# A differential-attention block: subtracting the two softmax maps in one step, and normalising the output per query in its own partition

## The chip, the cores and the metric

The kernel runs on one NeuronCore of a Trainium2 chip. The metric is the device time of one execution in microseconds (us). The engines named below are PE (TensorE: matmuls and transposes), DVE (VectorE), ACT (ScalarE), POOL (GpSimd) and SP (SyncE, which only issues DMAs here). Each engine takes its own list of instructions strictly in order.

## The reference

The program is one transformer block over 1024 tokens of width 1024: three attention branches (A: differential attention, B: dilated windows, C: attention to a memory), gates, an output projection and a feed-forward part. The change is in branch A, which has 4 heads; each head has two softmax maps over all 1024 keys, and values of width 128:

```
s = jnp.einsum('bqhcd,bkhcd->bhcqk', qb, k).astype(jnp.float32) * scale
s = s - slopes[None, :, None, None, None] * dist[None, None, None]
p = jax.nn.softmax(s, axis=-1)
p_diff = p[:, :, 0] - lam * p[:, :, 1]
return jnp.einsum('bhqk,bkhe->bqhe', p_diff.astype(v.dtype), v)
...
out_a = diff_attention(aq, ak, av, slopes_a, lam)
out_a = (rms_norm(out_a, a_subln[l]) * (1.0 - lambda_init)).reshape(b, t, BRANCH_WIDTH)
```

`rms_norm` divides each query's 128 outputs by the root of their mean square plus 1e-6, so a factor that is common to all outputs of a query only matters beside that 1e-6.

## The kernel before

The program runs in stages: the projections (to about 604 us of the profile), branch C (to about 685 us), branch A (about 685 to 1006 us), branch B (to about 1270 us), then mixing, output projection and feed-forward.

Branch A works on **steps**: one head and one block of 128 queries, 32 steps in all. Two steps (the index `e`) make a **pair** of 256 queries, 16 pairs in all. One step does this:

- For each of the two maps `m`: PE makes scores `sp` in two halves of 512 keys (L740, L741); three PSUM banks hold them. DVE adds the distance and takes the running minimum (L742), writing the row tile `s` (128 queries x 1024 keys). ACT takes the exponential in place and sums the row into `alc` (L746).
- DVE forms the reciprocals `arl` of both sums (L750) and multiplies the second by minus lambda, `nlam` (L751). POOL scales the second map by it (L752). DVE scales the first map and adds the second (L753).
- PE transposes the difference in 8 blocks into `tp` (L759); ACT, POOL and DVE split the transposed map into a high and a low part `pt` (L762, L765, L766, L768).

After both steps of a pair, PE multiplies with the values: 24 matmuls into the PSUM tile `op` (L773 to L775), with the 128 value columns in the partitions and the 256 queries along the row. The norm then needs a sum over partitions, per query. ACT copies `op` to `au` and squares it to `asq` (L778, L779). PE multiplies a matrix of ones with `asq`, so that each query's sum of squares stands in all 128 partitions (L781). The helper `rsqrt` takes its inverse root on tiles of 128x256: logarithm and exponential on ACT (L91, L92), one Newton step on DVE (L93 to L95). DVE multiplies `au` by it (L783), and a DMA stores `au` to DRAM (L784). `opp`, the pool that holds `op` and the sums of squares, has a single PSUM bank.

Between all this a filler runs: the gate projections, in units of 12 matmuls (tile `mm`, L191 to L193, called gate matmuls below), whose weights are loaded by SP, prepared by ACT and POOL (L210, L211), and whose results DVE takes out of PSUM (L542 to L574). The call `some_gates` releases one unit per step in branch A; a later stage takes what is left. A scheduler sets the final order of every engine's list when the program is built, and it may move instructions between neighbouring steps and stages; the lists are fixed after that.

At the start of branch B, SP loads three bias tables (L794) and then projected rows `nat` (L287), which PE transposes first (L293, 16 in a row). These loads stand behind the last store of `au` in SP's list.

Of the kernel before, what the change touches and what calls it, by code (L numbers as in the profile page):

```python
# [10 lines left out]
F32 = mybir.dt.float32  # L11
# [3 lines left out]
AF = mybir.ActivationFunctionType  # L15
ALU = mybir.AluOpType
# [4 lines left out]
P = 128  # L21
D = 1024
T = 1024
# [6 lines left out]
EPS = 1e-6  # L30
# [47 lines left out]
def hybrid_block_kernel(ctx: ExitStack, tc: tile.TileContext, xT, memT, w_ab, w_cq, w_kv,  # L78
                        w_gate, w_br, w_out, w_fg, w_fu, w_fd, pk_d, strip_d, bias0_d, bias1_d, bias2_d, out):
    nc = tc.nc  # L80
# [7 lines left out]
    def rsqrt(tp, val, n, shape, names, bufs=None):  # L88

        z, t = (tp.tile(shape, F32, name=m, bufs=bufs) for m in names)  # L90
        nc.scalar.activation(t, val, AF.Ln, bias=cst[:, {64: 0, 128: 1, D: 3}[n]:][:, :1])  # L91
        nc.scalar.activation(z, t, AF.Exp, bias=cst[:, 2:3], scale=-0.5)  # L92
        nc.vector.tensor_mul(t, z, z)  # L93
        nc.vector.scalar_tensor_tensor(out=t, in0=val, scalar=n * EPS, in1=t, op0=ALU.add, op1=ALU.mult)
        nc.vector.scalar_tensor_tensor(out=z, in0=t, scalar=1.5, in1=z, op0=ALU.subtract, op1=ALU.mult, reverse0=True)  # L95
        return z
# [7 lines left out]
    const = pool("const")  # L104
    ident = const.tile([P, P], F32, name="ident")
    make_identity(nc, ident)
    pk = const.tile([P, PK_COLS], F32, name="pk")
    nc.sync.dma_start(out=pk, in_=pk_d)
    cst = const.tile([P, 4], F32, name="cst")
    for i, v in enumerate((64 * EPS, 128 * EPS, -0.5 * math.log(2.0), D * EPS)):  # L110
        nc.vector.memset(cst[:, i:i + 1], v)
    ones = const.tile([P, P], F32, name="ones")
    nc.vector.memset(ones, 1.0)
# [4 lines left out]
    gk = const.tile([P, 8], F32, name="gk")  # L118
    for i, (a, b, dh) in enumerate(((PK_AQ, PK_AK, 64), (PK_BQ, PK_BK, 128), (PK_CQ, PK_CK, 128))):
        nc.vector.scalar_tensor_tensor(out=gk[:, i:i + 1], in0=pk[:, a:a + 1], scalar=-2.0 * float(dh) ** 0.5,  # L120
                                       in1=pk[:, b:b + 1], op0=ALU.mult, op1=ALU.mult)
# [9 lines left out]
    nlam = lams[:, 3:4]  # L131
# [38 lines left out]
    opp = pool("opp", 1, PSUM, att)  # L170
    small = pool("small", 3, stack=att)

    def ps_tile(pl, name):
        return pl.tile([P, 512], F32, name=name)
# [143 lines left out]
    with ExitStack() as pst:  # L318
# [61 lines left out]
        sq = sqs[0]  # L380
# [280 lines left out]
    with ExitStack() as st:  # L661
# [58 lines left out]
        for h in range(AH):  # L720
            QS, KA, KB = qk
            vH, vL = values(h)
            for pair in range(4):
                if h < AH - 1:
                    if pair == 0:
                        ahead = queries_keys(h + 1)
                    for _ in range(A_AHEAD[pair]):
                        qk = next(ahead)
                pts = [[ap.tile([P, 4, 256], F32R, name="pt", bufs=4) for _ in "HL"] for _ in range(2)]
                for e in range(2):  # L730
                    n = 2 * pair + e
                    off = (11 - (8 * (n % 2) + n // 2)) * 64
                    pr, lc = [], small.tile([P, 2], F32, name="alc")
                    for m in range(2):
                        tt = ap.tile([P, T], F32, name="s4", bufs=4)
                        nm = small.tile([P, 2], F32, name="anm")
                        for ch in range(2):
# [8 lines left out]
                        nc.scalar.activation(tt, tt, AF.Exp, bias=nm[:, 1:2], scale=-1.0, accum_out=lc[:, m:m + 1])  # L746
                        pr.append(tt)
                    some_gates(A_FIRST + (8 * h + 2 * pair + e + 1) * A_STEP, last, A_LAG)
                    rl = small.tile([P, 2], F32, name="arl")
                    nc.vector.reciprocal(rl, lc)  # L750
                    nc.vector.tensor_mul(rl[:, 1:2], rl[:, 1:2], nlam)  # L751
                    nc.gpsimd.tensor_mul(pr[1], pr[1], rl[:, 1:2].broadcast_to([P, T]))  # L752
                    nc.vector.scalar_tensor_tensor(out=pr[0], in0=pr[0], scalar=rl[:, 0:1], in1=pr[1],  # L753
                                                   op0=ALU.mult, op1=ALU.add)
                    for hf in range(2):
                        tp = ps_tile(tpp, "tp")
                        for k in range(4):
# [19 lines left out]
                sq = ap.tile([P, 256], F32, name="asq")  # L777
                nc.scalar.copy(u_, op)  # L778
                nc.scalar.activation(sq, op, AF.Square)  # L779
                ms_ = ps_tile(opp, "op")[:, :256]  # L780
                nc.tensor.matmul(ms_, lhsT=ones, rhs=sq, start=True, stop=True)  # L781
                y = rsqrt(ap, ms_, P, [P, 256], ("subz", "asq"))
                nc.vector.scalar_tensor_tensor(out=u_, in0=u_, scalar=gk[:, 3:4], in1=y, op0=ALU.mult, op1=ALU.mult)  # L783
                nc.sync.dma_start(out=spill[0][:, h, pair * 256:(pair + 1) * 256], in_=u_)  # L784


# [604 lines left out]
```

## Time and profile before

| | |
|---|---|
| median of 3 runs | 2114.03 us (2113.95 to 2117.42) |
| the profiled execution | 2113.94 us, its span 2112.2 us |
| busy share of the span | PE 94%, weight loads 81%, DVE 65%, POOL 53%, ACT 43% |
| PE idle over the span | 2112.2 - 1991.7 = 120.5 us |

Each engine's busy time is the union of its instructions' spans, so 100% would be an engine that never waits. Matmuls are pipelined: a 512-column matmul is shown as about 0.39 us long, while the next one starts 0.23 us after it. Shares over the whole span average over stages with different limits; branch A is about 15% of the span and is read by itself below. Times in the rows are counted from the span's start.

### The profile page before, as it was taken

To read this page: it belongs to the slowest core of one execution; us is meant where nothing else is said; L and a number is where in the kernel's file an instruction comes from. 1 tells how busy PE (TensorE), PEld (TensorE's weight loads), DVE (VectorE), ACT (ScalarE), POOL (GpSimd) and SP (SyncE) were. 2 spreads that over 40 slices of the span, in tenths; PEclk is the share of its full clock that TensorE was granted. 3 is DMA by queue.
4 is the path that set the end of the run, shared out by engine and by line. 5 is a ranking of instruction groups with operands and counts; after the bars stand their busy time and mean duration, and the time that the engine had idled before them with its cause. 6 is when DMAs were issued, how large, how long until landed. Compare 5 with 4: busy or idle time off the path is not lost. (4 is left out here: it accounts for less than half of the span.)

```text
span 2112.2 us, 31356 instructions
## 1 busy us (share of the span) xinstructions
PE 1991.7 (94%) x11384; PEld 1719.1 (81%) x11384; DVE 1367.5 (65%) x2144; ACT 917.2 (43%) x1839; POOL 1129.0 (53%) x770
## 2 busy tenths in 40 slices
PE   6799999999999889899989997999999999999999
PEld 5799999999977667678767785777788888888887
DVE  8975533566575799996354436733977667579961
ACT  4444322344444566664544555522523332344441
POOL 5686644666643576665355324810166454545754
PEclk9899999999999999999999998999999999999999
DMA  6263343323143333244856437632344323255442
GB/s 227 77 221 108 105 149 107 102 92 127 71 165 130 128 108 93 92 170 148 284 194 218 165 112 289 209 125 80 129 142 157 102 90 125 95 166 223 148 147 70
DMA packets 134730, 300.37 MB, mean 142 GB/s; under 512 B 19120, under 2 KB 43184, under 8 KB 134064
## 3 DMA queue, kind: packets, MB, share of 16 engines
q1 hardware_dynamic: 134576, 298.37, 41.9%
q8 instruction: 90, 1.47, 0.3%
q14 instruction: 64, 0.52, 0.1%
HBM read 204.58 MB, written 89.54 MB: 139 GB/s over the span
## 5 line engine op out<-in xcount | busy, mean ns | idle before, releaser
L211 POOL TENSOR_TENSOR wl<-raw,wh 128x512 fp32r<-128x512 f32 x204 | 282.2, 1396 | 190.8 <-ACT wh L210 167.2
L191 PE MATMUL pb<-t,wh 128*128 128x512 f32 x795 | 309.3, 391 | 15.6 <-DVE t L1100 14.5
L192 PE MATMUL pb<-t,wh 128*128 128x512 f32 x795 | 310.7, 391 | 1.9 <-DVE t L260 1.9
L193 PE MATMUL pb<-t,wl 128*128 128x512 f32 x795 | 310.4, 391 | 0.0
L191 PE MATMUL mm<-t,wh 128*128 128x512 f32 x657 | 266.0, 405 | 10.0 <-ACT wh L210 6.5
L192 PE MATMUL mm<-t,wh 128*128 128x512 f32 x657 | 261.1, 397 | 0.0
L193 PE MATMUL mm<-t,wl 128*128 128x512 f32 x657 | 260.0, 397 | 0.9 <-POOL wl L211 0.9
L210 ACT CAST wh<-raw 128x512 fp32r<-128x512 f32 x216 | 129.9, 618 | 199.4 <-PE pb L192 95.4
L191 PEld LDWEIGHTS pb<-t,wh 128*128 128x128 f32 x795 | 150.0, 189 | 47.9 <-DVE t L1100 14.9
L480 PE MATMUL sp<-wh,t 128*128 128x256 f32 x672 | 188.2, 280 | 0.0
L479 PE MATMUL sp<-wl,t 128*128 128x256 f32 x672 | 188.2, 280 | 0.0
L478 PE MATMUL sp<-wh,t 128*128 128x256 f32 x672 | 188.2, 280 | 0.0
L192 PEld LDWEIGHTS pb<-t,wh 128*128 128x128 f32 x795 | 150.1, 189 | 33.8 <-DVE t L260 2.4
L193 PEld LDWEIGHTS pb<-t,wl 128*128 128x128 f32 x795 | 150.2, 189 | 31.9 <-issue 0.5
L191 PEld LDWEIGHTS mm<-t,wh 128*128 128x128 f32 x657 | 125.3, 191 | 38.4 <-ACT wh L210 8.6
L193 PEld LDWEIGHTS mm<-t,wl 128*128 128x128 f32 x657 | 124.6, 190 | 27.6 <-POOL wl L211 1.3
L192 PEld LDWEIGHTS mm<-t,wh 128*128 128x128 f32 x657 | 125.4, 191 | 25.8 <-issue 0.5
L211 POOL TENSOR_TENSOR wl<-ws,wh 128x512 fp32r<-128x512 f32 x21 | 30.0, 1427 | 190.1 <-ACT wh L210 190.1
L465 POOL TENSOR_TENSOR wl<-ws,wh 128x512 fp32r<-128x512 f32 x72 | 99.2, 1401 | 59.5 <-ACT wh L464 46.3
L480 PEld LDWEIGHTS sp<-wh,t 128*128 128x128 f32 x672 | 127.8, 190 | 0.0
L478 PEld LDWEIGHTS sp<-wh,t 128*128 128x128 f32 x672 | 127.8, 190 | 0.0
L479 PEld LDWEIGHTS sp<-wl,t 128*128 128x128 f32 x672 | 127.8, 190 | 0.0
(439 smaller groups left out, 5346.4 us busy)
## 6 DMA issues: line engine op xcount, KB each, us to landing
proj<-nat SPq DMA_DIRECT2D x48, 512.0 KB, 2.8
raw<-in_w_gate SPq DMA_DIRECT2D x36, 512.0 KB, 3.5
nat<-proj SPq DMA_DIRECT2D x32, 512.0 KB, 4.2
raw<-in_w_fg SPq DMA_DIRECT2D x25, 512.0 KB, 3.6
raw<-in_w_fu SPq DMA_DIRECT2D x25, 512.0 KB, 4.0
raw<-in_w_ab SPq DMA_DIRECT2D x24, 512.0 KB, 3.8
rawp<-in_w_ab SPq DMA_DIRECT2D x24, 512.0 KB, 5.8
t<-in_w_fd SPq DMA_DIRECT2D x20, 512.0 KB, 7.0
```

What stands on the lines that cost most here:

```text
L191: nc.tensor.matmul(ps, lhsT=wh, rhs=rh, start=start, stop=False)
L192: nc.tensor.matmul(ps, lhsT=wh, rhs=rl, start=False, stop=False)
L193: nc.tensor.matmul(ps, lhsT=wl, rhs=rh, start=False, stop=stop)
L210: nc.scalar.copy(wh, src)
L211: low[0].tensor_sub(wl, src, wh.bitcast(F32))
L465: nc.gpsimd.tensor_sub(wl, r, wh.bitcast(F32))
L478: nc.tensor.matmul(ps[:, i], lhsT=aH, rhs=wh, start=k == 0, stop=False)
L479: nc.tensor.matmul(ps[:, i], lhsT=aH, rhs=wl, start=False, stop=False)
L480: nc.tensor.matmul(ps[:, i], lhsT=aL, rhs=wh, start=False, stop=k == 3)
```

## The change

Four things change, all in branch A.

1. The difference of the maps is made in units of the first map's sum. One reciprocal (of the second sum), one small operation that forms (first sum) x (-lambda) / (second sum), and one DVE instruction over 128x1024 that multiplies the second map by it and adds the first. The POOL multiplication is gone. The output is now larger by the first map's sum, per query.
2. The sums of both steps of a pair stand in one tile (`lcs`), because the norm needs the first ones: 1e-6 is multiplied by their square (`avs`).
3. The sum of squares is made with `asq` as the stationary operand and one column of ones, so that it stands per query in its partition: two matmuls of one column each. `rsqrt` then works on 128x2 instead of 128x256.
4. The factor is put back along the row by two PE transposes of a broadcast column into a third tile of the same `opp` bank (`yb`), which the last multiplication reads from PSUM.

```diff
-                    rl = small.tile([P, 2], F32, name="arl")
-                    nc.vector.reciprocal(rl, lc)
-                    nc.vector.tensor_mul(rl[:, 1:2], rl[:, 1:2], nlam)
-                    nc.gpsimd.tensor_mul(pr[1], pr[1], rl[:, 1:2].broadcast_to([P, T]))
-                    nc.vector.scalar_tensor_tensor(out=pr[0], in0=pr[0], scalar=rl[:, 0:1], in1=pr[1],
-                                                   op0=ALU.mult, op1=ALU.add)
+                    rl = small.tile([P, 1], F32, name="arl")
+                    nc.vector.reciprocal(rl, lc[:, 1:2])
+                    nc.vector.scalar_tensor_tensor(out=rl, in0=lc[:, 0:1], scalar=nlam, in1=rl, op0=ALU.mult, op1=ALU.mult)
+                    nc.vector.scalar_tensor_tensor(out=pr[0], in0=pr[1], scalar=rl, in1=pr[0], op0=ALU.mult, op1=ALU.add)
...
-                ms_ = ps_tile(opp, "op")[:, :256]
-                nc.tensor.matmul(ms_, lhsT=ones, rhs=sq, start=True, stop=True)
-                y = rsqrt(ap, ms_, P, [P, 256], ("subz", "asq"))
-                nc.vector.scalar_tensor_tensor(out=u_, in0=u_, scalar=gk[:, 3:4], in1=y, op0=ALU.mult, op1=ALU.mult)
+                ms_ = ps_tile(opp, "op")[:, :2]
+                for e in range(2):
+                    nc.tensor.matmul(ms_[:, e:e + 1], lhsT=sq[:, e * P:(e + 1) * P], rhs=ones[:, :1], start=True, stop=True)
+                vs_ = small.tile([P, 2], F32, name="avs")
+                nc.vector.scalar_tensor_tensor(out=vs_, in0=lcs[:, :, 0], scalar=P * EPS, in1=lcs[:, :, 0], op0=ALU.mult, op1=ALU.mult)
+                nc.vector.tensor_add(vs_, ms_, vs_)
+                y = rsqrt(small, vs_, 0, [P, 2], ("az", "aw"))
+                yb = ps_tile(opp, "op")[:, :256]
+                for e in range(2):
+                    nc.tensor.transpose(out=yb[:, e * P:(e + 1) * P], in_=y[:, e:e + 1].broadcast_to([P, P]), identity=ident)
+                nc.vector.scalar_tensor_tensor(out=u_, in0=u_, scalar=gk[:, 3:4], in1=yb, op0=ALU.mult, op1=ALU.mult)
```

The scheduler's order changes with it, at three places that matter below. Lines of the changed kernel are a few higher (L755 there is L753 here, L774 is L773, L793 is L783, L794 is L784, L804 is L794).

PE at the end of branch A in the kernel before: the last product of `op`, 22 gate matmuls, the sum of squares, 50 more gate matmuls, and then the first transposes of branch B.

```order
L775 MATMUL op<-pt,vL 128x256
...
L781 MATMUL op<-asq,ones 128x256
...
L293 MATMUL tp<-ident,nat 128x128 x16
L876 MATMUL sp<-bkT,bqT 128x192
L876 MATMUL sp<-bkT,bqT 128x256 x6
L876 MATMUL sp<-bkT,bqT 128x192
L293 MATMUL tp<-ident,nat 128x128 x16
```

The same place in the changed kernel; `az` is the factor per query, and L792 its transposes.

```order
L776 MATMUL op<-pt,vL 128x256
...
L784 MATMUL op<-ones,asq 128x1 x2
...
L792 MATMUL op<-ident,az 128x128 x2
L293 MATMUL tp<-ident,nat 128x128 x16
L886 MATMUL sp<-bkT,bqT 128x192
L886 MATMUL sp<-bkT,bqT 128x256 x3
```

Here 14 gate matmuls stand ahead of the sums of squares, 22 between them and the transposes of the factor, and none between those and branch B's first transposes. Twelve gate matmuls follow after the last row shown. Counted over the whole list, 792 gate matmuls stand ahead of branch B's first transposes, 720 before.

PE in the changed kernel, in the fourth pair: what stands around the transposes of the factor (three pairs of 16 look like this one, a fourth has two score matmuls in between instead; in the others more work stands between the two).

```order
L742 MATMUL sp<-ka,qs 128x512
L743 MATMUL sp<-kb,qs 128x512
L760 MATMUL tp<-ident,s_9150 128x128 x4
L792 MATMUL op<-ident,az 128x128 x2
L760 MATMUL tp<-ident,s_9150 128x128 x4
L774 MATMUL op<-pt,vH 128x256
```

Only four transposes of the next map stand between L792 and the next product into `op`, which can begin when L793 on DVE has read the bank.

SP at the same end of the stage, before: the last store of `au` (`spill<-au`), two weight loads of the filler, the bias tables, and the rows that PE transposes first.

```order
L575 DMA gate_7129<-raw 128x512
L784 DMA spill_58<-au 128x256
L559 DMA raw<-in_w_gate 128x512
L560 DMA raw<-gatep_7147 128x512
L794 DMA bias_11170<-in_bias 128x256
L794 DMA bias_11171<-in_bias 128x512
L794 DMA bias_11172<-in_bias 128x128
L287 DMA nat<-proj_135 128x1024 x2
```

In the changed kernel one load less stands between the store and branch B's rows; the store is still ahead of them.

```order
L575 DMA gate_7133<-raw 128x512
L794 DMA spill_58<-au 128x256
L559 DMA raw<-in_w_gate 128x512
L804 DMA bias_11235<-in_bias 128x256
L804 DMA bias_11236<-in_bias 128x512
L804 DMA bias_11237<-in_bias 128x128
L287 DMA nat<-proj_136 128x1024 x2
```

## Rows read from the trace of the kernel before

**Rows 1.** Busy time of each engine in five stretches: projections and C, branch A from its start to its last scores, A's tail, branch B, and the turn after B. Columns: stretch, its length, then busy us of PE, weight loads, DVE, ACT and POOL (with instructions), the granted PE clock, the DMA share and GB/s.

```profile
core 0: us, PE busy (x) PEld busy (x) DVE busy (x) ACT busy (x) POOL busy (x), PEclk, DMA share, GB/s
0.00:684.00 684.00, 644.63 (x5015) 615.48 (x5016) 424.90 (x660) 272.67 (x562) 405.67 (x283) 0.98 0.37 129
685.00:968.00 283.00, 252.27 (x1328) 205.09 (x1327) 251.56 (x491) 182.81 (x341) 184.28 (x112) 0.97 0.37 117
968.00:1006.40 38.40, 34.96 (x184) 29.49 (x182) 19.99 (x32) 10.82 (x22) 20.46 (x15) 1.00 0.51 181
1006.40:1270.00 263.60, 243.50 (x1320) 202.35 (x1321) 111.96 (x303) 138.37 (x394) 112.50 (x83) 0.97 0.59 192
```

**Rows 2.** Who waited for whom between 680 and 1000 us: waiting engine and line, what ended the wait, total us, times, longest.

```profile
POOL s L752 <- DVE arl L751: 42.5, 24, 6.3
ACT s L746 <- DVE anm L742: 40.9, 30, 5.1
PEld sp L740 <- DVE anm L742: 21.9, 33, 2.6
PE sp L740 <- DVE anm L742: 11.8, 17, 2.4
```

**Rows 3.** DVE's groups between 685 and 1000 us, by line and shape: count, busy us, mean ns of one, then the idle time before them.

```profile
L753 DVE SCALAR_TENSOR_TENSOR s<-s,arl,s 128x1024 f32<-128x1024 f32 x32 | 61.6, 1926 | 11.7 <-POOL s L752 11.3
L742 DVE CUSTOM_DVE_ANT_0 s<-sp,strip,anm 128x512 f32<-128x512 f32 x64 | 47.2, 743 | 1.8
L95 DVE SCALAR_TENSOR_TENSOR subz<-asq,subz 128x256 f32<-128x256 f32 x16 | 16.2, 1012 | 0.2
L783 DVE SCALAR_TENSOR_TENSOR au<-au,gk,subz 128x256 f32<-128x256 f32 x16 | 14.7, 918 | 0.1
L93 DVE TENSOR_TENSOR asq<-subz 128x256 f32<-128x256 f32 x16 | 11.1, 695 | 1.0 <-ACT subz L92 1.0
L751 DVE TENSOR_TENSOR arl<-arl,lams 128x1 f32<-128x1 f32 x32 | 9.8, 305 | 0.4
L94 DVE SCALAR_TENSOR_TENSOR asq<-op,asq 128x256 f32<-128x256 f32 x16 | 6.7, 418 | 0.2
```

**Rows 4.** The same view, 685 to 968 us only: the large subtraction with the wait ahead of it, and POOL's multiplication over the whole of A (685 to 1000 us).

```profile
L753 DVE SCALAR_TENSOR_TENSOR s<-s,arl,s 128x1024 f32<-128x1024 f32 x31 | 60.3, 1947 | 9.6 <-POOL s L752 9.2
...
L752 POOL TENSOR_TENSOR s<-s,arl 128x1024 f32<-128x1024 f32 x32 | 66.3, 2073 | 47.3 <-DVE arl L751 42.5 <-PE op L775 3.7 <-PE sp L741 0.7
```

**Rows 5.** Durations of single lines over the whole trace: count, then shortest/median/longest ns, first and last start in us.

```profile
L753 DVE SCALAR_TENSOR_TENSOR s<-s,arl,s x32: 1271/2274/3365, 708.1 to 973.7; 128x1024 f32<-128x1024 f32 x32
L94 DVE SCALAR_TENSOR_TENSOR asq<-op,asq x16: 411/418/425, 737.6 to 994.7; 128x256 f32<-128x256 f32 x16
L94 DVE SCALAR_TENSOR_TENSOR n8w<-ss,n8w x28: 152/168/1823, 106.0 to 599.6; 128x8 f32<-128x8 f32 x28
L94 DVE SCALAR_TENSOR_TENSOR mw<-tp,mw x1: 151/151/151, 27.5 to 27.5; 128x2 f32<-128x2 f32 x1
```

**Rows 6.** DVE's small operations of `rsqrt` in the stretch 0 to 684 us, which read their tensors from SBUF: count, busy us, mean ns.

```profile
L93 DVE TENSOR_TENSOR n8w<-n8z 128x8 f32<-128x8 f32 x28 | 15.2, 543 | 5.1 <-ACT n8z L92 5.0
L95 DVE SCALAR_TENSOR_TENSOR n8z<-n8w,n8z 128x8 f32<-128x8 f32 x28 | 14.7, 525 | 0.8
L94 DVE SCALAR_TENSOR_TENSOR n8w<-ss,n8w 128x8 f32<-128x8 f32 x28 | 13.8, 493 | 0.6
```

**Rows 7.** Instructions in order of time around one large subtraction: start us, length us, engine, line, operation, tiles.

```profile
784.15 2.42 POOL L678 TENSOR_TENSOR vL<-nat,vH 128x1024 fp32r<-128x1024 f32 x1
784.28 3.37 DVE L753 SCALAR_TENSOR_TENSOR s<-s,arl,s 128x1024 f32<-128x1024 f32 x1
786.68 2.10 POOL L211 TENSOR_TENSOR wl<-raw,wh 128x512 fp32r<-128x512 f32 x1
```

**Rows 8.** PE's small parts: the one-column matmuls that the kernel has elsewhere (over the trace), four transposes and the two passes of the sum of squares in order of time.

```profile
L385 PE MATMUL tp<-ones,nat x4: 167/250/250, 23.1 to 23.3; 128*128 128x1 f32 x4
...
786.47 0.60 PE L759 MATMUL tp<-ident,s 128*128 128x128 f32 x4
786.90 0.60 PE L781 MATMUL op<-asq,ones 128*128 128x256 f32 x2
```

**Rows 9.** The end of branch A in order of time, PE, DVE and SP (SPq: a DMA being issued).

```profile
990.71 0.60 PE L781 MATMUL op<-asq,ones 128*128 128x256 f32 x2
996.61 0.92 DVE L783 SCALAR_TENSOR_TENSOR au<-au,gk,subz 128x256 f32<-128x256 f32 x1
997.56 0.32 SPq L784 DMA_DIRECT2D spill<-au  x1
999.08 0.43 SPq L560 DMA_DIRECT2D raw<-gatep  x1
1001.04 0.85 SPq L287 DMA_DIRECT2D nat<-proj  x2
1003.48 0.39 PE L193 MATMUL mm<-t,wl 128*128 128x512 f32 x1
1006.46 3.57 PE L293 MATMUL tp<-ident,nat 128*128 128x128 f32 x16 [2.59 <-DMA nat<-proj]
```

More of the change, by code (lines that the diff above doesn't have):

```diff
@@ L90, in rsqrt @@
         z, t = (tp.tile(shape, F32, name=m, bufs=bufs) for m in names)
-        nc.scalar.activation(t, val, AF.Ln, bias=cst[:, {64: 0, 128: 1, D: 3}[n]:][:, :1])
+        nc.scalar.activation(t, val, AF.Ln, bias=cst[:, {64: 0, 128: 1, D: 3, 0: 4}[n]:][:, :1])
         nc.scalar.activation(z, t, AF.Exp, bias=cst[:, 2:3], scale=-0.5)
@@ L108, in hybrid_block_kernel @@
     nc.sync.dma_start(out=pk, in_=pk_d)
-    cst = const.tile([P, 4], F32, name="cst")
-    for i, v in enumerate((64 * EPS, 128 * EPS, -0.5 * math.log(2.0), D * EPS)):
+    cst = const.tile([P, 5], F32, name="cst")
+    for i, v in enumerate((64 * EPS, 128 * EPS, -0.5 * math.log(2.0), D * EPS, 0.0)):
         nc.vector.memset(cst[:, i:i + 1], v)
@@ L729, in hybrid_block_kernel @@
                 pts = [[ap.tile([P, 4, 256], F32R, name="pt", bufs=4) for _ in "HL"] for _ in range(2)]
+                lcs = small.tile([P, 2, 2], F32, name="alc")
                 for e in range(2):
@@ L732, in hybrid_block_kernel @@
                     off = (11 - (8 * (n % 2) + n // 2)) * 64
-                    pr, lc = [], small.tile([P, 2], F32, name="alc")
+                    pr, lc = [], lcs[:, e]
                     for m in range(2):
```

## The prediction

> **What bounds the kernel now.** The page says PE is busy for 94% of the span, so I looked first for the stretch in which PE waits, with the busy times by stretch [rows 1]. In branch A up to its last scores (685 to 968 us) PE is busy 252.3 of 283 us and DVE 251.6: PE has 30.7 us of idle time, and DVE, with 89%, has hardly more room. ACT and POOL are at 65%. The table of waits tells which of the two sets the pace [rows 2]: the largest waits that end at PE's score matmuls (L740, 21.9 us in the weight loads and 11.8 us in the matmuls, which overlap) are for DVE's L742 to give a score bank back, and ACT waits 40.9 us for the same line. PE waits for DVE, so here an us of DVE time is worth about 1/0.889 us of the stage. After 968 us (the tail) and in branch B it is PE that is full (91 and 92%) and DVE is about half busy; DVE time saved there is worth nothing.
>
> Next, what DVE does in A [rows 3]. The subtraction L753 takes 61.6 us, 1.926 us each, though its shortest takes 1.271 [rows 5]. One of the long ones shows why: L753 takes 3.37 us where POOL's L678 had started 0.13 us before it, and ends only about 1 us after the next POOL instruction started [rows 7]. So a DVE instruction that reads two tensors from SBUF loses time to POOL. L94, which reads one of its tensors from PSUM, never does: 411 to 425 ns in all 16 [rows 5].
>
> **What the change removes and adds on DVE.** Per pair the norm's L93, L94, L95 and L783 cost 0.695 + 0.418 + 1.012 + 0.918 = 3.04 us, 48.7 us in all; L751 costs 9.8 us [rows 3]. In their place stand, per pair, five operations on 128x2 and the last multiplication, and per step one operation on 128x1.
>
> - The last multiplication now reads the factor from PSUM, as L94 does its tensor: 0.418 x 16 = 6.7 us. The addition of the sums from PSUM is like the 128x2 operation at 151 ns [rows 5]: 2.4 us.
> - Four operations per pair and one per step read two small tensors from SBUF: 64 + 32 = 96 in all. This price, p, decides the case. Below it is bounded by the undisturbed 151 ns [rows 5] and above by the waits of today's larger ones (L95: 1.012 - 0.41 = 0.60 us of waiting, so p = 0.75). Nearest are the 128x8 operations of the projections: 0.493 to 0.543 us [rows 6] with a shortest of 0.15, so 0.37 us of waiting, while POOL was busy 405.7 of 684 us, 59% [rows 1]. POOL loses L752, 66.3 us [rows 4], so in A it falls from 204.7 us to 138.4 of some 300, 46%. In proportion: 0.15 + 0.37 x 0.46/0.59 = 0.44 us. I take that; 96 x 0.44 = 42.2 us.
> - L753 stays in number and shape. Its 0.655 us of waiting shrinks at best to nothing (20.9 us less) and at worst not at all, since it never overlapped its own L752. In proportion to POOL's share (0.64 to 0.46) it loses 0.18 us, 5.8 us in all.
>
> DVE: 6.7 + 2.4 + 42.2 - 48.7 - 9.8 - 5.8 = -13.0 us. Some 13.5 of the 16 pairs end before the tail, so 84% of it counts: -10.9, and divided by 0.889 -12.3 us of the stage.
>
> The Trainium skill (SBUF — State Buffer, section "Who interferes with whom") says of this contention that it is an exclusive lock on a port pair, held for a whole instruction, taken by a DVE instruction with two SBUF inputs against a GpSimd one that reads SBUF. By that rule a wait doesn't shrink with the operand, and making the norm's tiles small saves only their own length; with the waits that L95 has now the sum would come out as in the third rival. The rows on L94 and the 128x8 operations agree with the rule; how often a small operation here will meet POOL they don't tell.
>
> **POOL's multiplication as a wait.** DVE stood still 9.2 us before L753 because POOL had not finished L752 [rows 4]. That wait goes: -9.2 us. What is late next is DVE itself, since the second operand then comes from ACT, one step earlier.
>
> **PE and ACT.** Per pair PE loses two passes of 256 columns (0.60 us as shown) and gets four passes of one column (0.23 us shown, but each with a weight load) and two transposes (half of 0.60 us) [rows 8]: about +0.25 us, 4 us in all. The 30.7 us of idle PE time before the tail hide it; without that cover it costs 4 us. ACT's two instructions get shorter; ACT is at 65% and the gain is nothing.
>
> **The end of the stage.** Branch B's first rows stand behind the last store of `au` on SP, and the last store waits for the last multiplication. Today that ended at 996.61 + 0.92 = 997.53, SP issued the store at once, then two loads and three tables, the rows at 1001.04, and PE could go on at 1006.46: 8.9 us after the multiplication. PE filled that with 50 gate matmuls and was idle for 2.6 us [rows 9]. In the new order only 22 stand after the sums of squares, then the transposes of the factor, then nothing until the rows of B are there. The multiplication ends about 1 us after those transposes (0.42 and two handovers), and the rows come 8.9 - 0.4 us later, one load less being ahead of them: 9.5 us idle instead of 2.6, +7 us. The gate matmuls that stood here are done later: PE idles 20.1 us in B [rows 1], part of which they can fill. Against that, 72 more gate matmuls (by the order) stand ahead of B than before, which fill A's tail and leave B with fewer to cover its own waits. I put the two together at +2.5 us, an eighth of B's idle time; bounds 0 and +5.
>
> **Sum.** -12.3 - 9.2 + 7 + 2.5 = -12.0. The profiled execution took 2113.94 us, the median is 2114.03: 2102 us.
>
> **The rivals.**
>
> *POOL's contention nearly goes.* With p at 0.15 and L753 at its shortest DVE saves 55 us. Then PE is the bound: the stage can lose only the 30.7 us of PE idle time, and -30.7 + 9.5 gives 2093. PE's busy time is of pipelined spans, so some of it may close as well; I allow 7 us more, 2086. For it speaks that POOL loses a third of its work in A, against it that what remains (L211, L766) is what L753 meets today.
>
> *The gain is handed on.* p as the 128x8 operations show it unscaled (0.52) leaves 5 us from DVE; with the wait for POOL 14 us; the end of the stage takes 9.5 back, and the bank of `op` may take the rest. The bank is now held through three tiles: the next product waits for the transposes of the factor and the multiplication behind them. In four pairs only 4 transposes or 2 score matmuls stand between, so PE waits there for 0.42 us and perhaps one L742 (0.74 [rows 3]) ahead of it on DVE, 1.2 us: 4.6 us. Time: 2110 to 2114.
>
> *Slower: the small operations wait as long as the large ones did.* With p = 0.75 the 96 cost 72 us, L753 gains nothing, and DVE has 22.6 us more work than now. Times 0.84/0.889 that is +21.4; -9.2 and +9.5 give 2136. The point from which this decides is p = 0.57, where the sum is zero (L753 gaining its 5.8 us); at 0.62 the kernel is 0.2% slower. The 128x8 operations at 0.52 are close to it; that POOL is less busy speaks against.
>
> **How the numbers follow.** A measurement of this kernel can tell about 0.2%, 4.2 us, from no change. Forecast (2090 to 2109): 0.50. Contention gone (below 2090): 0.17. Handed on (2110 to 2118): 0.18. Slower (above 2118): 0.15. So faster 0.67, same 0.18, slower 0.15. The range 2086 to 2118 leaves out most of the slower case and the far end of the better one; the forecast's own range is 2090 to 2109.
>
> **What would show it.** In the changed kernel's profile: POOL's 66 us of L752 gone; the 128x2 operations at about 0.44 us, and L755 (was L753) at about 1.75; no DVE wait for POOL ahead of it; the stretch to the last scores about 20 us shorter (5 us more of it by work moved into the tail); and a PE wait of about 9 us for `nat` at the start of B. The prediction is wrong if p comes out under 0.3 or over 0.57, if PE's waits move to the transposes of the factor and the products behind them, or if B's wait is not there.

## The result, and the profile after

| | before | after |
|---|---|---|
| median | 2115.73 us | 2138.01 us (2137.47 to 2139.98) |
| ratio | | 1.0108, 95% interval 1.0092 to 1.0124 |
| profiled execution: span | 2112.2 us | 2135.8 us |

The kernel became 1.1% slower; 2102 us had been forecast. In the changed file the lines of branch A are two to ten further down: L742 is the score product, L744 DVE's minimum, L748 the exponential, L755 the large subtraction, L763 to L769 the split into `pt`, L774 to L776 the products with the values, L793 the last multiplication.

Busy times of the changed kernel by stretch (columns as in [rows 1]): up to A, A up to its last scores, A's tail, and as much of B as [rows 1] shows.

```profile
0.00:691.00 691.00, 651.83 (x5032) 622.26 (x5033) 420.16 (x664) 276.20 (x565) 403.70 (x284) 0.99 0.37 128
692.00:959.00 267.00, 239.03 (x1309) 197.40 (x1308) 219.70 (x505) 173.21 (x327) 109.79 (x78) 0.97 0.38 122
959.00:1035.60 76.60, 61.97 (x322) 50.95 (x320) 30.45 (x55) 20.56 (x43) 38.73 (x31) 0.96 0.50 171
1035.60:1299.20 263.60, 236.48 (x1278) 197.56 (x1279) 96.77 (x296) 134.70 (x387) 95.19 (x70) 0.95 0.54 174
```

From the first score product to the start of the last (the **score part**) A took 275.4 us and takes 266.9. The **tail**, from there to B's first transposes, took 42.7 us and takes 76.7. A begins 3.6 us later, and what follows B's start is 5.6 us shorter: 3.6 - 8.5 + 34.0 - 5.6 = +23.5, the difference of the spans. So the gain in the score part is smaller than forecast, and the tail grew by four times as much.

Part of that is work that only changed its place. PE's idle time (length minus PE busy) shows what was lost. Before, in score part, tail and all that follows:

```profile
688.36:963.84 275.48, 244.75 (x1293) 198.89 (x1293) 245.03 (x479) 177.75 (x333) 179.60 (x109) 0.97 0.37 118
963.84:1006.46 42.62, 39.12 (x203) 32.94 (x201) 24.11 (x41) 13.89 (x28) 23.86 (x17) 1.00 0.46 163
1006.46:2112.20 1105.74, 1058.87 (x4856) 868.20 (x4856) 670.80 (x962) 450.26 (x913) 518.53 (x360) 0.98 0.47 155
```

In the changed kernel the first two are the second and third row of the table further up; the third is:

```profile
1035.63:2135.79 1100.16, 1044.29 (x4784) 857.10 (x4784) 657.61 (x954) 445.18 (x904) 500.21 (x345) 0.98 0.45 150
```

PE's idle time fell by only 2.8 us in the score part (30.7 to 28.0), and grew by 11.1 in the tail (3.5 to 14.6) and by 9.0 after B's start (46.9 to 55.9).

DVE did get lighter (251.56 us in [rows 1], now 219.70) and POOL too. Its groups between 690 and 960 us, columns as in [rows 3]:

```profile
L755 DVE SCALAR_TENSOR_TENSOR s<-s,arl,s 128x1024 f32<-128x1024 f32 x31 | 42.8, 1381 | 0.7
L754 DVE SCALAR_TENSOR_TENSOR arl<-alc,lams,arl 128x1 f32<-128x1 f32 x31 | 16.7, 537 | 0.6
L793 DVE SCALAR_TENSOR_TENSOR au<-au,gk,op 128x256 f32<-128x256 f32 x12 | 5.7, 475 | 1.1 <-PE op L792 1.0
L93 DVE TENSOR_TENSOR aw<-az 128x2 f32<-128x2 f32 x13 | 5.2, 403 | 0.2
L95 DVE SCALAR_TENSOR_TENSOR az<-aw,az 128x2 f32<-128x2 f32 x13 | 4.1, 319 | 0.2
```

The subtraction fell from 1.947 to 1.381 us [rows 4], and DVE's wait for POOL ahead of it is gone. What is new stands in the table of waits (690 to 985 us, columns as in [rows 2]):

```profile
ACT s L748 <- DVE anm L744: 33.7, 32, 6.3
...
ACT pt L763 <- PE op L775: 21.2, 11, 6.6
...
PEld sp L742 <- DVE anm L744: 13.6, 16, 1.8
```

ACT's casts into `pt` wait 21.2 us for products that still read the old `pt`: the products come late. Why, one pair shows. The products of this pair ended at 809.64 us and its squares at 811.50; then, in order of time:

```profile
814.98 0.50 PE L784 MATMUL op<-ones,asq 128*128 128x1 f32 x4
817.73 0.15 DVE L787 TENSOR_TENSOR avs<-op,avs 128x2 f32<-128x2 f32 x1
820.42 0.16 DVE L95 SCALAR_TENSOR_TENSOR az<-aw,az 128x2 f32<-128x2 f32 x1
822.21 0.38 PE L792 MATMUL op<-ident,az 128*128 128x128 f32 x2
822.29 1.28 DVE L755 SCALAR_TENSOR_TENSOR s<-s,arl,s 128x1024 f32<-128x1024 f32 x1
823.61 0.48 DVE L793 SCALAR_TENSOR_TENSOR au<-au,gk,op 128x256 f32<-128x256 f32 x1
824.14 0.19 PEld L774 LDWEIGHTS op<-pt,vH 128*128 128x128 f32 x1 [1.35 <-DVE au L793]
824.15 0.38 PE L774 MATMUL op<-pt,vH 128*128 128x256 f32 x1 [1.11 <-DVE au L793]
```

The single bank of `op` holds the products, then the sums, then the factor. It comes free at 824.09 us with the last multiplication, 14.5 us after the products ended, and the next pair's first product starts 0.06 us later. The instructions of the chain are each 0.15 to 0.5 us long; the rest is turns in the queues of PE, DVE and ACT. By the times of eleven pairs in the middle of A, the bank is taken (from the first product to the last read) for 16.8 us of a period of 17.9 us, and no next product starts before the last multiplication has ended. Before, the bank came free with L94, and the next products started on average 1.7 us before the last multiplication ended:

```profile
775.71 0.41 DVE L94 SCALAR_TENSOR_TENSOR asq<-op,asq 128x256 f32<-128x256 f32 x1
777.07 0.28 PE L773 MATMUL op<-pt,vH 128*128 128x256 f32 x1
777.89 0.91 DVE L783 SCALAR_TENSOR_TENSOR au<-au,gk,subz 128x256 f32<-128x256 f32 x1
```

But the bank was nearly full before too. By the same count it was taken for 16.5 us of a period of 18.0. With the new subtraction and the old norm (subtraction_alone below) it is 15.6 of 16.2: there the bank leaves almost no room, and the new norm holds it 1.2 us longer per pair. (The hold is no fixed length: a pair's products themselves spread over 5.0 us of it before and 5.1 in subtraction_alone, and over 3.2 now; from the last product to the last read it grew from 11.5 and 10.5 to 13.6 us.)

The end of A, with columns as in [rows 9]:

```profile
1025.32 0.38 PE L792 MATMUL op<-ident,az 128*128 128x128 f32 x2
1026.13 0.48 DVE L793 SCALAR_TENSOR_TENSOR au<-au,gk,op 128x256 f32<-128x256 f32 x1
1026.63 0.40 SPq L794 DMA_DIRECT2D spill<-au  x1
1028.24 0.33 SPq L559 DMA_DIRECT2D raw<-in_w_gate  x1
1028.61 1.38 SPq L804 DMA_DIRECT2D bias<-in_bias  x3
1030.09 0.85 SPq L287 DMA_DIRECT2D nat<-proj  x2
1035.63 3.86 PE L293 MATMUL tp<-ident,nat 128*128 128x128 f32 x16 [9.93 <-DMA nat<-proj]
```

### The profile page after: what moved, and what is told of

Its sections match the earlier page's. It is cut to its first block, busy times and chain, and to the rows that moved or that the text cites. A ratio compares the mean times of both kernels' runs of the same rounds, so it can differ in the third digit from the quotient of the medians.

```text
span 2135.8 us, 31452 instructions
## 1 busy us (share of the span) xinstructions
PE 1998.1 (94%) x11448; PEld 1728.5 (81%) x11448; DVE 1328.5 (62%) x2177; ACT 915.6 (43%) x1839; POOL 1052.7 (49%) x738
## 4 chain that ended last, share of the span: by engine, by line
PE 73%; DVE 8%; DMA 5%; issue 3%; ACT 2%; POOL 2%; SPq 1%; POOLq 0%; ACTq 0%; DVEq 0%
PE pb L191 8%; PE pb L193 8%; PE pb L192 8%; PE mm L191 6%; PE mm L193 6%; PE mm L192 6%; PE sp L480 4%; PE sp L478 4%; PE sp L479 4%; PE mm L480 2%; PE mm L478 2%; PE mm L479 2%; PE tp L293 1%; PE op L479 1%; PE op L480 1%
## 5 line engine op out<-in xcount | busy, mean ns | idle before, releaser
L465 POOL TENSOR_TENSOR wl<-ws,wh 128x512 fp32r<-128x512 f32 x72 | 96.4, 1361 | 64.1 <-ACT wh L464 51.2
L479 PE MATMUL mm<-wl,t 128*128 128x256 f32 x448 | 126.1, 282 | 0.0
```

Of the source, the lines that this page charges most:

```text
L465: nc.gpsimd.tensor_sub(wl, r, wh.bitcast(F32))
L479: nc.tensor.matmul(ps[:, i], lhsT=aH, rhs=wl, start=False, stop=False)
```

## The experiments

The theory after the result was **bank**: the new norm costs time because the products' only bank is held through the whole chain. Rivals were **operations** (the many small operations cost it by themselves), **border** (what is lost is lost between A and B) and, when A's later start had been seen, **place** (where the added tiles push all others).

**The two halves apart.** subtraction_alone takes the changed lines L730 to L755 with the old norm; its 1e-6 is not multiplied by the first sum's square, so that small part of the computation is left out. norm_alone takes the rest with the old subtraction (the 1e-6 then as in the old norm).

> The one-step subtraction with the old norm (its 1e-6 is then not scaled by the square of the first sum; all else is computed). By the order, 720 gate matmuls stand ahead of branch B's first transposes, 48 of them after the last sum of squares, as in the kernel before (720, 50). Theory 'border' (the loss of the full change comes from the norm, which changes the order at the end of branch A): the tail and B cost what they did, and the stretch to the last scores gains what it gained in the full change or a little more, 5 to 12 us: 2103 to 2110 us. Theory 'DVE' (an us of DVE time is worth an us of branch A, as predicted): L753 at about 1.4 us instead of 1.93 gives 17 us, the small operation takes 5 back, the wait for POOL gives 9: 2092 to 2096. Theory 'bank' says nothing against either.

Measured: 2094.57 us, ratio 0.9886 (0.9869 to 0.9903), as theory 'DVE' had it. Its score part, its tail and what follows (columns as above):

```profile
688.30:942.20 253.90, 237.22 (x1293) 197.09 (x1292) 228.64 (x481) 179.62 (x335) 115.28 (x80) 0.98 0.40 128
942.20:986.66 44.46, 39.29 (x202) 32.63 (x201) 22.19 (x39) 12.87 (x26) 19.60 (x15) 0.99 0.47 161
986.66:2092.89 1106.23, 1060.06 (x4856) 868.89 (x4856) 672.58 (x962) 450.55 (x913) 521.50 (x360) 0.98 0.47 155
```

> The old subtraction with POOL, and the new norm on 128x2 (without the scaling by the first sum, which isn't needed then). By the order 792 gate matmuls stand ahead of B's first transposes, 36 of them after the transposes of the factor, so the wait for B's first rows is covered. Theory 'border': 72 gate matmuls (16.6 us of PE) moved ahead of B, of which B gives back 5: +11, less what DVE saves: 2118 to 2126. Theory 'bank' (one bank held through three tiles delays each pair): branch A itself is longer, 10 to 20 us: 2124 to 2134, with waits of PE for au L793 and az L95. Theory 'DVE': 24 us less DVE work, 2095 to 2105.

Measured: 2144.56 us, ratio 1.0127 (1.0104 to 1.0150), more than any of its forecasts. The subtraction gives 22 us, all in the score part (275.4 to 253.9). The norm takes 28 us alone and 43 beside the new subtraction: the whole error is the norm's. The 28 are not waits alone: norm_alone starts A 8 us later than before (place, below), and its score part has a granted clock of 0.93, where before has 0.97.

Changed kernel minus subtraction_alone, in their profiles: start +3.7, score part +13.0, tail +32.2, rest -6.0, together +42.9. In PE's idle time it is +11.3 in the score part, +9.5 in the tail and +9.7 after B's start, 30.5 in all; the other 12.4 us are PE busy for longer, 3.7 of them ahead of A.

**The border.** lag_four sets `B_LAG` from 8 to 4 in the changed kernel, by which 708 gate matmuls stand ahead of B instead of 792; store_from_pool issues the last store of `au` from POOL:

```
-nc.sync.dma_start(out=spill[0][...], in_=u_)
+(nc.gpsimd if h == AH - 1 and pair == 3 else nc.sync).dma_start(out=spill[0][...], in_=u_)
```

> The full change; only the constant that lets branch B's gate units run ahead (B_LAG, 8) is 4. PE's order up to the last scores is the same as in the changed kernel, row for row; 708 gate matmuls stand ahead of B instead of 792, and none after the last product of op. Theory 'border': the 84 matmuls go back into B, where their 19 us replace idle time as before (gain 11 to 13), but the last norm and the wait for B's rows stand uncovered (3 to 5 us more): 2126 to 2132. Theory 'bank': the delay is in the pairs before the tail, so nothing is gained: 2136 to 2143.

> The changed kernel with the last store of A's outputs issued from POOL's queue instead of SP's, so that B's first rows no longer stand behind it on SP; all other stores as they were. Theory 'border': PE's wait for nat ahead of B falls from 9.9 to under 3 us and B starts some 7 us earlier, total 2128 to 2133. Rival 'given back': B starts earlier but runs into its own later loads, or the gates' loads that stand behind are late instead: total 2136 to 2141.

Both took longer than either of their forecasts. Measured: lag_four 2149.74 us (ratio 1.0148, 1.0129 to 1.0167): the tail fell from 76.7 to 62.4 us, but what follows grew by 27. The 84 gate matmuls are some 19 of these (at 0.23 us each), and its granted clock was lower, 0.975 over the span against 0.981. store_from_pool 2144.98 us (1.0134, 1.0112 to 1.0156): the wait for `nat` stayed at 11.3 us, because on SP the gates' loads and stores, which wait themselves, took the store's place ahead of B's rows. Neither is a remedy; the border theory in its simple form (take away the gates, or the store, and the time is back) fell.

**Place.** before_shifted and after_realigned only move tiles; the order on every engine is the same but for one memset:

```
-small = pool("small", 3, stack=att)
+small = pool("small", 3, stack=att); nc.vector.memset(small.tile([P, 72], F32, name="pad", bufs=1), 0.0)
```

(72 columns in before; 56 in the changed kernel.)

> The kernel before with one tile more of 288 bytes per partition among the small tiles, filled once at the start and never read: every tile that is allocated behind the small ones stands 288 bytes higher, as in the changed kernel, and on every engine the order of the instructions is the same but for that one memset. Theory 'place': in the changed kernel the projections ahead of A ran slower not because of their own work but because of where their operands stand: the 1582 matmuls from 175 to 600 us that take their stationary operand from the moved tiles started every 113.33 ns in the trace of before and every 116.76 ns in that of the changed kernel, those with an operand that did not move every 120.0 and 119.9 ns. Expected then: 116.8 ns here too, first scores of A at 692 instead of 688.4 us, total 3 to 6 us above before (2119 to 2122). Rival 'other': the delay comes with the new norm itself (the clock, or transfers): 113.3 ns, 688.4 us, total within 2 us of before.

> The changed kernel with a never-read tile of 224 bytes among the small ones, so that the tiles behind stand 512 bytes higher than in before instead of 288; the order on every engine is the same but for the memset that fills it. Theory 'place' (what counts is the address modulo 64 to 256 bytes): stationary operands at 113.3 ns, first scores at 688.4 instead of 692.0 us, total 3 to 6 us under the changed kernel (2132 to 2135). Rival 'other': 116.8 ns, 692 us, 2136 to 2140.

Measured: before_shifted ratio 1.0029 (1.0019 to 1.0039), some 6 us slower; after_realigned 2134.16 us, 1.0071 (1.0054 to 1.0087) where the changed kernel had 1.0108, so 4 us less by the medians and 8 by the ratios. In their traces the projections' 256-column products with a moved stationary operand start every 116.76 and 113.33 ns, as in the changed kernel and in before. A stretch in which PE is full at a granted clock of 1.00, the 2.4 GHz level, shows it in the number of matmuls: before, changed, before_shifted, after_realigned.

```profile
300.00:470.00 170.00, 170.00 (x1455) 170.00 (x1454) 88.22 (x130) 59.27 (x110) 96.42 (x71) 1.00 0.32 108
```

```profile
300.00:470.00 170.00, 170.00 (x1437) 170.00 (x1436) 84.72 (x126) 57.92 (x106) 94.28 (x69) 1.00 0.32 109
```

```profile
300.00:470.00 170.00, 170.00 (x1437) 170.00 (x1436) 84.30 (x125) 57.92 (x106) 94.19 (x69) 1.00 0.33 111
```

```profile
300.00:470.00 170.00, 170.00 (x1454) 170.00 (x1453) 88.07 (x131) 59.80 (x111) 96.30 (x71) 1.00 0.32 108
```

An attempt to use it failed:

> The kernel of subtraction_alone with the same two tiles (192 bytes ahead of the hidden rows' tiles, 64 bytes among the small ones, so that all else stands 256 bytes higher); the order on every engine is that of subtraction_alone but for the two memsets. Theory 'place': the 1970 products of the projections at 113.3 to 114 ns instead of 120.0, A's first scores at 670 to 677 instead of 688.3 us, total 2072 to 2084 (subtraction_alone 2094.6). Rival 'moved operand only': 120 ns as before, 688 us, total 2092 to 2098.

Measured: 2111.9 us (0.9970, 0.9950 to 0.9991), 17 us slower than subtraction_alone. All projection products, those at 120.0 as well as those at 113.3 ns, now took 117.8 on average, and 16 us were lost after B's start. So the distance of the two operands modulo 256 bytes is not the rule; the rule stays open.

**Another bank for the norm's tiles.** other_bank puts sums and factor into the transposes' two banks, factor_in_scores_bank the factor into one of the scores' three:

```
-yb = ps_tile(opp, "op")[:, :256]
+yb = ps_tile(spp, "sp")[:, :256]
```

> The changed kernel with the sums of squares and the transposed factor in the two banks of the score transposes (tpp) instead of the one bank of the products (opp); the scheduler orders the rest anew. Theory 'bank': in the changed kernel the next pair's products wait until the last multiplication has read the factor out of the products' only bank; the casts into pt wait for the products (21.2 us in 11 waits in the score part, 8.0 us where only the subtraction was changed), Exp is late, and the score part takes 266.9 us where the subtraction alone had 253.9. Expected then: casts' wait under 10 us, score part 254 to 260 us, total 2124 to 2131. Rival 'chain': the part is longer because of the norm's longer chain of small operations through five engines, whatever bank: score part 265 to 269 us, total 2135 to 2140.

> The changed kernel with one thing else: the transposed factor is written into one of the scores' three banks (spp) instead of the products' only one (opp); the sums of squares stay where they were. The scheduler orders the rest anew: 720 gate matmuls stand ahead of B as in before, not 792, and after the last scores only one pair's products, not three. Theory 'bank': what the new norm costs beside the new subtraction (some 43 us) is mostly that the products' bank is held until the factor is read, by which products, casts and exponentials are late and gates and a pair's products are left over between A and B. Expected then: casts' wait for products under 5 us in the score part (15.5 in the changed kernel), score part 250 to 258 us, last score to B under 50 us (76.7), total 2098 to 2112. Rival 'chain': the longer chain of small operations costs it by itself, and three score banks with one held as long as the factor is read delay the scores instead, as the two transposes' banks did: score part over 264 us, total 2130 or more.

Measured: other_bank 2187.72 us (1.0326), score part 318.8; factor_in_scores_bank 2258.28 us (1.0662), score part 423.8, tail 38.7. (scores_bank_and_place, the second one with tiles moved much as in subtraction_and_place, took 2272.14 us, where 14 to 25 less than without the move had been the theory.) The theory's forecast was wrong in both; of the rivals the second one's ('2130 or more') held. In the second PE itself stands before the transposes of the factor and of the maps (score part, columns as in [rows 2]):

```profile
PE tp L760 <- DVE s L755: 48.7, 15, 4.5
PE sp L792 <- DVE az L95: 26.7, 15, 2.3
PE op L784 <- ACT asq L780: 16.1, 15, 2.3
```

The scheduler had given these another order, so the two runs don't tell what a bank alone is worth; they show only that, in these orders, the factor costs more among banks that the next step needs sooner.

**Who holds the bank.** no_factor drops the transposes of the factor, factor_unread keeps them; in both the last multiplication reads the squares instead (`in1=yb` becomes `in1=sq`).

> The changed kernel without the two transposes that write the factor into the products' bank; the last multiplication takes the squares in the factor's place, so the outputs are not normalised. The sums of squares, the eight small operations on DVE and ACT behind them and the last multiplication remain, but nothing waits for their result, and the bank is free as soon as the sums are read. Theory 'bank' (what the new norm costs is that PE and the bank wait for the factor at the end of the chain): score part 254 to 260 us (266.9 in the changed kernel, 253.9 with the subtraction alone), last score to B 40 to 58 us (76.7 and 44.5), total 2098 to 2114. Rival 'operations' (the small operations cost it, by DVE's and ACT's time and by standing ahead of others in their queues): score part 264 to 270 us, total 2126 to 2138.

> As no_factor, but the two transposes of the factor stand where they were: the products' bank is taken until they are done, and only the last multiplication does not read them (it takes the squares, so the outputs are not normalised). Theory 'bank': nearly all the price is back, since the bank and PE wait for the chain's end and the multiplication adds one operation to that: score part 262 to 268 us, total 2122 to 2138. Rival 'reader' (the price is the last multiplication behind the factor, on the way to the store): as no_factor within 6 us.

Measured: no_factor 2115.45 us (0.9991, 0.9979 to 1.0003), factor_unread 2111.27 us (0.9964, 0.9950 to 0.9978). The price is not in the transposes, and most of it not in the small operations, which are all still there: 27 of the 43 us go when the last multiplication no longer reads the factor. This was the rival "reader"; theory 'bank' as put there, with the price in the wait of PE and bank up to the transposes, was refuted. In factor_unread the score part is 260.5 us and the tail 56.2, and PE no longer waits for `nat` at B's start, since the store too no longer waits for the chain. So the 27 us are not the bank's alone: of the 24.8 us of PE idle time that go, 8.4 lie in the score part, 9.9 are the wait for `nat`, and 7.3 lie after B's start (0.8 come on ahead of A). no_factor had 686 gate matmuls ahead of B and factor_unread 756, with B starting at 988 and 1011 us and nearly the same end: there, gates moved across the border cost nothing that can be seen. From 756 to the changed kernel's 792 nothing came back: 1099.5 and 1100.2 us from B's start to the end.

**A second bank.** `spp` from 3 to 2 and `opp` from 1 to 2, in the changed kernel and in subtraction_alone:

> The changed kernel with two banks for the products and two for the scores instead of one and three. To be read against two_banks_subtraction, which has the same banks and the old norm. Theory 'bank': with a second bank the next pair's products need not wait for the factor, so that the new norm costs 5 to 20 us here (both minus subtraction), where it costs 43 with one bank. Rival 'operations': 35 to 50 us here too. The two banks of the scores may cost or give something of their own, in both kernels alike: totals 2080 to 2150.

> The kernel with the new subtraction alone (and the old norm), with two banks for the products and two for the scores: the control of two_banks_both. It tells what a bank moved from the scores to the products is worth by itself: 2094.6 with one and three; expected within 25 us of that, since the scores' third bank covers DVE's minima (PE waited 4.2 us for them in the score part of subtraction_alone) and the products' second one covers the sums of squares.

Measured: 2126.82 us (1.0041, 1.0025 to 1.0058) and 2121.69 us (1.0021, 1.0005 to 1.0037). The norm costs 5 us here, place included, where it costs 43 with one bank. PE's idle time over the span tells the same: 121.4 us with the new norm and 121.8 with the old, against 137.7 and 107.3 with one bank. The waits of ACT's casts for products are no longer among ACT's nine largest, and the next products start 2.2 us before the last multiplication ends. Giving a bank of the scores to the products costs 27 us with the old norm, 9.5 of them ahead of A, and the new norm gets back 11 (2138.01 to 2126.82). One reserve: a score part that is slower for another reason (277.8 us) also hides more.

**An earlier reader.** On top of after_realigned, with the whole computation kept:

```
+nc.scalar.copy(sq, yb)
-nc.vector.scalar_tensor_tensor(out=u_, in0=u_, scalar=gk[:, 3:4], in1=yb, ...)
+nc.vector.scalar_tensor_tensor(out=u_, in0=u_, scalar=gk[:, 3:4], in1=sq, ...)
```

> The kernel of after_realigned (2134) with one operation more: ACT copies the factor from the products' bank into the squares' tile in SBUF, and the last multiplication on DVE reads that copy. All is computed as in the changed kernel. Theory 'reader' (the bank comes free when the last multiplication has read it, and that stands in DVE's queue behind minima and subtractions of 1.1 to 1.4 us; without that read the kernel was 27 us faster): ACT reads the factor sooner, the next pair's products start sooner, total 2108 to 2126. Rival 'queue of ACT': ACT's copy stands behind an exponential and casts of its own and frees the bank no sooner, and ACT carries 16 copies more: total 2132 to 2145.

Measured: 2118.43 us, ratio 1.0004 (0.9990 to 1.0018), 16 us under after_realigned, level with before, and 24 above subtraction_alone. One pair in order of time:

```profile
812.00 0.38 PE L792 MATMUL op<-ident,az 128*128 128x128 f32 x2
812.98 0.37 ACT L793 COPY asq<-op 128x256 f32<-128x256 f32 x1
813.90 0.19 PEld L774 LDWEIGHTS op<-pt,vH 128*128 128x128 f32 x1
814.13 0.28 PE L774 MATMUL op<-pt,vH 128*128 128x256 f32 x1
814.33 0.48 DVE L794 SCALAR_TENSOR_TENSOR au<-au,gk,asq 128x256 f32<-128x256 f32 x1
```

The products start before DVE's multiplication. The two profiled executions differ by 23 us, more than the medians: 3 in the score part (264.3 to 261.2), 11 in the tail (78.1 to 67.0) and 8.5 after B's start. In the tail the new order put gates behind the factor's transposes, and the wait for `nat` fell from 10.8 to 1.4 us: most of what is gained there is this wait. factor_by_pool, which also gave the multiplication to POOL, took 2129.9 us (1.0054), between its two forecasts.

One more run missed its aim: more_dve_before was to add DVE work in A of the old kernel, but the scheduler put the added reductions at the program's start (4 to 75 us). It took 2137.36 us and says nothing on A; that this is what its theory 'DVE' had forecast is chance.

## Why the prediction was wrong

- **DVE sets the pace of A: right. The gain there: right in the half that the subtraction is.** The forecast for PE's gain in the score part was -12.3 - 9.2 = -21.5 us. The subtraction alone shortened it by exactly that, but this is luck: by the forecast's own prices the subtraction was worth some 11 us there (9.8 - 14.1 + 5.8 = 1.5 us of DVE, and the wait of 9.2), and the rest was the norm's. With the lengths in the table above (L755 0.57 us shorter than L753, not 0.18; L754 0.54 us, not 0.44) the same working gives 21 us for it. So the mechanism was right and the sizes were not; the norm's share came out as a loss.
- **The price p: inside its bounds.** It was 0.44 us in the forecast; the 85 such operations of the score part take 0.375 on average. In norm_alone, where POOL keeps its multiplication and is busy for 59% of the score part instead of 41%, L93 and L95 take 0.708 and 0.492 us, against 0.403 and 0.319 here: p does go with POOL's load. The wait does not shrink with the operand: L754, on one column, takes 220 ns as a median and 1299 at worst; on average that is 0.33 us over its shortest, and L755 with 1024 columns, right behind it, loses 0.11. This is what the Trainium skill (SBUF — State Buffer, "Who interferes with whom") says of a lock held for a whole instruction, and the trace agrees.

```profile
L754 DVE SCALAR_TENSOR_TENSOR arl<-alc,lams,arl x32: 211/220/1299, 707.3 to 964.6; 128x1 f32<-128x1 f32 x32
```

- **The bank of `op`: the step that failed.** The sum put it at nothing. The rival "handed on" named it ("the next product waits for the transposes of the factor and the multiplication behind them") and priced it at 4.6 us, by PE's wait at the product where little stands between. PE is indeed idle for only 1.9 us at the products behind the multiplication. But the bank was taken for 16.5 of 18.0 us already before the change, and with the new subtraction alone it is 15.6 of 16.2: by these counts a norm that holds it 1.2 us longer has to lengthen the period. The products come later in PE's list, and ACT's casts wait for them: 21.2 us. The score part became 8.5 us shorter instead of 21.5, PE's idle time in it fell by 2.8, and over the span the new norm added some 30 us of it with one bank and none with two.
- **The 72 gate matmuls: mis-sized.** The term was +2.5 us. At 0.23 us each they are 16.6 us of the tail, and what follows became only 5.6 us shorter: PE's idle time there grew by 9.0 us. How much of this is the gates' is not shown: with the same 792 ahead of B factor_copied idles 49.3 us there, and lag_four with 708 idles 54.3, so their number alone does not decide it. With them came one more pair's products and transposes, and 3.5 us of small PE waits for the gates' own weights, by the trace.
- **The wait for B's rows: right.** Forecast 9.5 us idle, measured 9.93.
- **Place: missing.** Three added small tiles of 96 bytes cost some 4 to 8 us far from A. Nothing in the prediction looked there.
- **The signs** named ahead did show it in part: p was inside its bounds and the wait at B was there, but the stretch to the last scores was 8.5 us shorter and not 20, L755 took 1.38 us and not 1.75, and the products behind the factor had become the wait, though under ACT's name and not PE's.
- **Near by luck.** The third rival's 2136 us is close to the measured time, but it came from p = 0.75 and a subtraction that gains nothing, and neither was so.

Not settled: how the 13 us that the norm adds to the score part divide between the bank and the small operations. factor_unread and factor_copied still have 6.6 and 7.3 us more there than subtraction_alone. And the scheduler made another order in each of these kernels, so the runs show what a bank or a reader is worth together with the order that follows from it. No run frees the bank with the changed kernel's order kept, and none tells which of the losses in the tail and after B's start come from the late bank and which from the order alone.

## What to carry to other kernels

Price a tile that takes the same bank again by the time from the first write to the last read, with a turn in the queue for every engine that its chain passes, and compare it with the period at which the bank is wanted; the lengths of the instructions say little. Do this for the kernel before the change too: here 16.5 of 18.0 us were taken, and that could be read from its trace. If the last reader sits in a busy queue, try letting another engine copy the tile out first (16 us here). A bank that is wanted too often may not show as a wait under its own name: here PE was idle for 1.9 us at the products, while ACT's casts waited 21.2 us. And count PE's idle time by stage, not only the stages' lengths, where a scheduler moves work from one to the next.

## What the runs showed of the hardware

The pace of back-to-back 256-column products depends on where their operands stand in SBUF: the projections' products whose stationary operand moved start every 113.3 ns in before, 116.8 in the changed kernel, 118.7 in norm_alone and 117.8 in subtraction_and_place, all at a granted clock of 1.00; those with operands that did not move start every 120.0 ns, until they too were moved (117.8 in subtraction_and_place). The tiles were moved by 192 to 512 bytes. The pace was the same in every run with the same placing, on different chips: 113.3 in before and subtraction_alone (and in factor_copied, with the tiles 512 bytes higher), 116.8 in the changed kernel, lag_four and two_banks_both. A tile that is never read, put among the small ones, cost 0.3% of the whole program in one kernel and gave some 0.2 to 0.4% in another.
